# HGRN state in three groups, one query buffer, the gate row ahead of the norm's factor, and stores on SyncE in a two-layer backbone kernel

## The chip, the core and the metric

The kernel runs on one core of a Trainium2 chip. The core has TensorE (PE, matmuls into PSUM banks), VectorE (DVE), ScalarE (ACT), GpSimd (POOL) and SyncE (SP, which here issues DMAs), each with its own instruction stream; semaphores order them. The metric is the device time of one execution in microseconds (us); less is better. The profile is a recording of one such execution.

## The reference

The network has two layers on 512 latent tokens and 256 context tokens of width 1024, all float32. Layer 0 mixes tokens by bidirectional retention, layer 1 by HGRN2; each is followed by a ConvGLU channel mixer of hidden width 2816. Around every sub-layer stand two RMSNorms, and a shift, scale and gate from a condition vector (`mod`):

```python
u_l = rms_norm(h_l, norm_g[i, 0]) * (1.0 + sc1_l) + sh1_l
y_l = mixer(u_c, u_l, ...)
h_l = h_l + g1_l * rms_norm(y_l, norm_g[i, 1])
u_l = rms_norm(h_l, norm_g[i, 2]) * (1.0 + sc2_l) + sh2_l
h_l = h_l + g2_l * rms_norm(conv_ffn(u_l, ...), norm_g[i, 3])
```

HGRN2 has 8 heads of width 128. In each direction a state of 128x128 follows `S_t = diag(a_t) S_{t-1} + k_t v_t^T`, and the output is `o_t = S_t^T q_t`, context first, then latents from the context's last state; the outputs of both directions are summed. `q` is `silu` of a projection, `k` and `a` come from a sigmoid of another. Only the latents are returned, so layer 1 needs no context output.

## The kernel before

Matmuls are float32 in three passes: each operand is split into a high and a low part (`h..` by ScalarE's copy, `l..` by a subtraction on VectorE, line 94), and high x high, high x low and low x high are summed in PSUM. Weights come by DMA from SP into two raw buffers (`r..`), two high and two low ones. Activations `u` (`um`, `ue`) are kept transposed, features on the partitions. The stages are: retention with layer 0, its FFN, HGRN (about 1300 to 1740 us of the span), the second FFN (about 1800 to 2100), and an end.

PSUM has eight banks in two pools: six for projections and accumulation ("mm"), two for small products ("sc"). The order of PE's instructions is the program's order for the whole kernel. VectorE's and ScalarE's order is set by a scheduler when the kernel is built, except in the tails, below.

**HGRN.** `attend(h)` computes one head and yields weights; `weave` puts PE work of the next head's projections (for head 7: of `out1`, the output projection of heads 0 to 3) between its steps, a fixed number of columns (83000, for head 7 64000) by the weights, 37 in all. A head forms `A` (decay) and `K` for six blocks of 128 tokens, `Q` for both directions, the products of decays over 2, 4, ... 128 tokens (`T`, on GpSimd), and in seven levels `li` scales halves of `Q` and `K` by them (line 1209), copies them to `L` and multiplies them on PE (`hl`, line 1216) into the block-diagonal matrix `DG`. `hd` and line 1194 start `DG`. Then come the states: ten transposes of `K` (`ht`, copied to `KT` by ScalarE), ten products with `v` (`hc`, line 1240), each read by VectorE, which copies the first of a direction (`s`, line 1245) and chains the others (`S`, line 1248). They go in groups of 4, 1, 4, 1 through the two small banks. Last, `ho` sums over the four latent blocks the matrix part (line 1253) and both directions' state parts (1254, 1255), and `hn` starts the norm.

`Q` has two buffers, so the scheduler may begin the next head's `Q` (direction 0 on VectorE, line 1174; direction 1 on GpSimd, 1175) while this head's `ho` is not done. `k0`, the sum of both directions' `K`, is on GpSimd (1172).

**Tails.** Each stage ends in `tail`: the last output projection (`tl`), then `handover`, which per block of 128 tokens evacuates (line 421), squares and sums (424), forms the factor r (428 and a Newton step on VectorE), multiplies by r and the gate row `g` (448), adds to the residual `h` (451), forms the second norm's factor, scales (457, 459), transposes on PE in pairs of blocks (`tre`, `trm`, 473), modulates on ScalarE (482) and splits into u (489, 490). `tail` also holds the next stage's first projections (`ld`) in units of 24 matmuls. All steps are given to a `Plan` with an engine, a cost, dependencies and a rank; `Plan.run` simulates them on four engines with these costs and emits them in the order found, and for ScalarE and VectorE that order is kept. The last tail has no next stage: it works by halves of 512 columns (443, 445) and stores each half (446). `filler(n)` emits a part of the condition's modulation vectors, 16 matmuls `ada`, taken from a queue; the rest of the queue is done in the second FFN.

## Time and profile before

| | |
|---|---|
| median of 3 runs | 2158.03 us (2157.18 to 2159.58) |
| profiled execution | 2157.03 us, span 2155.3, granted clock 0.993 |
| busy: PE, DVE, ACT, POOL | 2096.5, 1340.6, 840.0, 304.5 us |
| PE busy in the span's 1300 to 1740 us (HGRN) | 418.99 of 440 us |
| PE busy in 1740 to 1800 us (HGRN's tail) | 53.63 of 60 us |
| PE busy in 1240 to 1300 us (first FFN's tail) | 60.00 of 60 us |

A row of the timeline has the start, the duration, the engine with the line, the operation, output and inputs, and the number of instructions that it stands for; brackets hold the idle time of the engine before it and what ended that. ACTq is ScalarE's queue of instructions that it issues but doesn't compute, DMAs among them. A row with x8 is eight instructions one after the other.

### The profile page before, as it was taken

The numbers are of one execution on the slowest core, as the hardware profiler recorded it, in microseconds if no ns is written. First come the engines' busy times: TensorE is split into PE (matmuls) and PEld (weight loads), VectorE is DVE, ScalarE is ACT, GpSimd is POOL, SyncE is SP. The second block draws the span as 40 slices with busy tenths as digits, with TensorE's granted clock in tenths as the row PEclk, the third lists the DMA queues.
The fourth block names the chain that finished last, engine by engine and source line by source line (L and its number), as shares of the span: only waits on it lengthen the run. The fifth ranks groups of instructions, "written<-read, shape, count | busy, mean of one in ns | idle before, by whom it ended". The sixth has DMA issues, their size and how long they took to land. (4 is left out here: it accounts for less than half of the span.)

```text
span 2155.3 us, 30784 instructions
## 1 busy us (share of the span) xinstructions
PE 2096.5 (97%) x12288; PEld 1767.7 (82%) x12288; DVE 1340.6 (62%) x2536; ACT 840.0 (39%) x1631; POOL 304.5 (14%) x383
## 2 busy tenths in 40 slices
PE   6999999999999999999999999999999889999997
PEld 5888888888888988888888889888888668888886
DVE  6866565663613777467676577777777765334545
ACT  5542342433523723322132166444443454333323
POOL 4622040310100000000000003333333310000000
PEclk9999999999999999999999999999999999999999
DMA  9122314234133223333333532212121253223232
GB/s 299 40 79 96 110 40 139 68 98 147 49 108 127 100 98 110 126 115 125 113 101 122 190 100 86 59 40 60 40 60 40 79 186 121 79 98 98 93 117 93
DMA packets 186608, 218.24 MB, mean 101 GB/s; under 512 B 6112, under 2 KB 157664, under 8 KB 185696
## 3 DMA queue, kind: packets, MB, share of 16 engines
q1 hardware_dynamic: 179280, 196.80, 27.9%
q0 software_dynamic: 2736, 13.11, 1.6%
q10 hardware_dynamic: 4448, 6.35, 0.9%
q8 instruction: 97, 1.59, 0.3%
q14 instruction: 47, 0.39, 0.1%
HBM read 200.90 MB, written 15.34 MB: 100 GB/s over the span
## 5 line engine op out<-in xcount | busy, mean ns | idle before, releaser
L121 PE MATMUL f<-um,hua 128*128 128x512 f32 (+1 forms) x960 | 258.2, 357 | 0.0
L121 PE MATMUL f<-um,huv 128*128 128x512 f32 (+1 forms) x960 | 255.9, 354 | 0.0
L264 DVE SCALAR_TENSOR_TENSOR rows<-rada,sc,rows 128x256 f32<-128x256 f32 x504 | 232.0, 485 | 5.4
L1059 PE MATMUL f<-hd,gt 128*128 128x512 f32 x720 | 228.3, 396 | 0.0
L121 PEld LDWEIGHTS f<-um,hua 128*128 128x128 f32 x960 | 169.7, 189 | 29.2 <-issue 3.8
L121 PE MATMUL hp<-ue,hhw 128*128 128x512 f32 (+1 forms) x672 | 192.1, 373 | 0.0
L121 PEld LDWEIGHTS f<-um,huv 128*128 128x128 f32 x960 | 170.1, 189 | 25.1
L121 PE MATMUL f<-um,lua 128*128 128x512 f32 (+1 forms) x480 | 170.2, 355 | 0.0
L121 PE MATMUL f<-um,luv 128*128 128x512 f32 (+1 forms) x480 | 169.9, 354 | 0.0
L1059 PEld LDWEIGHTS f<-hd,gt 128*128 128x128 f32 x720 | 135.1, 188 | 33.5 <-issue 0.8
L1059 PE MATMUL f<-ld,gt 128*128 128x512 f32 x360 | 142.3, 395 | 0.0
L121 PEld LDWEIGHTS hp<-ue,hhw 128*128 128x128 f32 x672 | 112.0, 190 | 17.8 <-issue 1.4
L817 PE MATMUL v<-hv,ua 128*128 128x512 f32 x384 | 120.6, 391 | 0.0
L121 PE MATMUL hp<-ue,lhw 128*128 128x512 f32 (+1 forms) x336 | 120.2, 358 | 0.0
L121 PEld LDWEIGHTS f<-um,lua 128*128 128x128 f32 x480 | 90.8, 189 | 13.0
L121 PEld LDWEIGHTS f<-um,luv 128*128 128x128 f32 x480 | 90.8, 189 | 12.6
L1031 DVE TENSOR_TENSOR c<-f,c 128x512 f32<-128x512 f32 (+1 forms) x60 | 36.1, 602 | 99.7 <-PE f L121 98.8
L985 PE MATMUL wo<-hwo,ogr 128*128 128x512 f32 x288 | 89.4, 391 | 0.0
L1018 ACT ACTIVATE c<-f,c_conv_b,c_conv_w 128x512 f32<-128x512 f32 (+1 forms) x60 | 42.1, 702 | 117.4 <-PE f L121 117.4
L817 PEld LDWEIGHTS v<-hv,ua 128*128 128x128 f32 x384 | 72.1, 188 | 15.3 <-issue 0.6
L93 ACT ACTIVATE hua<-rua 128x512 fp32r<-128x512 f32 x80 | 44.2, 621 | 102.2 <-DMA rua<-ffn_w_up 53.2
L451 POOL DMA_DIRECT2D h_dram<-hxe x6 | 3.2, 532 | 570.6 <-DVE yf L421 536.9
(503 smaller groups left out, 4820.7 us busy)
## 6 DMA issues: line engine op xcount, KB each, us to landing
rada<-ada_w SPq DMA_DIRECT2D x48, 1024.0 KB
rua<-ffn_w_up SPq DMA_DIRECT2D x20, 1024.0 KB
ruv<-ffn_w_up SPq DMA_DIRECT2D x20, 1024.0 KB
rd<-ffn_w_down SPq DMA_DIRECT2D x24, 768.0 KB
rhw<-hg_w_in SPq DMA_DIRECT2D x28, 512.0 KB
rv<-ret_w_in SPq DMA_DIRECT2D x8, 1024.0 KB
rg<-ret_w_in SPq DMA_DIRECT2D x8, 1024.0 KB
rqk<-ret_w_in SPq DMA_DIRECT2D x6, 1024.0 KB
```

The costliest lines, as they stand in the source:

```text
L93: self.nc.scalar.activation(hi, raw, AF.Copy)
L121: nc.tensor.matmul(o, a, b[:, s], start=(i == 0), stop=(i == n - 1))
L264: nc.vector.scalar_tensor_tensor(rows[:, v], raw[:, k], a, rows[:, v], ALU.mult, ALU.add)
L451: nc.vector.tensor_tensor(hb(b), hb(b), yb(b), ALU.add), nc.gpsimd.dma_start(hdst[ts], hb(b))))
L817: nc.tensor.matmul(ps, a, b, start=(c == 0 and k == 0 and z == 0), stop=(c == 1 and k == 3 and z == 2))
L985: nc.tensor.matmul(ps, l, r[:, k], start=(h == 0 and k == 0 and z == 0), stop=(h == 2 and k == 3 and z == 2))
L1018: nc.scalar.activation(c[:, s], ps, AF.Identity, bias=cb[:, i, mt : mt + 1], scale=w(1))
L1031: nc.vector.tensor_tensor(c[:, s], ps, c[:, s], ALU.mult)
L1059: nc.tensor.matmul(ps, l, r[:, k], start=(k1 + k == 0 and z == 0), stop=(k1 + k == nt - 1 and z == 2))
```

## The change

Six edits stand in the diff.

1. `handover`: two products of y with the gate row, 512 columns each, stand ahead of the factor r, and one operation `h = y*r + h` behind it, in place of `y*r*g` and an add. In the last tail this is by halves.
2. The last tail's stores are issued by SyncE.
3. In `attend` `Q` has one buffer, and one VectorE operation of 1024 columns forms both directions.
4. The states go in three groups: four of direction 0, four of direction 1, then the fifth of both. ScalarE copies them in three steps, the yields are 1, 1, 2, and `ho` takes the latent blocks in the order 1, 2, 3, 0 and direction 1 ahead of 0.
5. `out1` calls `filler` once, in its second half, and no longer twice. What it leaves comes in the second FFN's first unit.
6. The low parts of the last output weights (`lhwt`) are made by VectorE in place of GpSimd.

```diff
--- before.py
+++ after.py
@@ -436,19 +436,19 @@
                                                                             ALU.add))
             n = add("ACT", 0.28, [n], (-1,), lambda: start(r, ss[0][:, 2:3]))
             n = add("DVE", 0.55, [n], (-1,), lambda: self.newton(r[0], ss[0][:, 2:3]))
+            yg = [add("DVE", 0.69, [sq[c]], (pr, 1), lambda cs=half(c): nc.vector.tensor_tensor(
+                yb(b)[:, cs], yb(b)[:, cs], g[:, v, cs], ALU.mult)) for c in range(2)]
             if u is None:
                 for c in range(2):
                     cs = half(c)
-                    n = add("DVE", 1.35, [n], (pr, 2), lambda cs=cs: (
-                        nc.vector.scalar_tensor_tensor(yb(b)[:, cs], yb(b)[:, cs], r[0][:, 0:1], g[:, v, cs],
-                                                       ALU.mult, ALU.mult),
-                        nc.vector.tensor_tensor(hb(b)[:, cs], hb(b)[:, cs], yb(b)[:, cs], ALU.add),
-                        (nc.sync, nc.scalar)[c].dma_start(hdst[ts, cs], hb(b)[:, cs])))
+                    n = add("DVE", 0.75, [n, yg[c]], (pr, 2), lambda cs=cs: (
+                        nc.vector.scalar_tensor_tensor(hb(b)[:, cs], yb(b)[:, cs], r[0][:, 0:1], hb(b)[:, cs],
+                                                       ALU.mult, ALU.add),
+                        nc.sync.dma_start(hdst[ts, cs], hb(b)[:, cs])))
                 return None
-            n = add("DVE", 1.28, [n], (pr, 2), lambda: nc.vector.scalar_tensor_tensor(
-                yb(b), yb(b), r[0][:, 0:1], g[:, v], ALU.mult, ALU.mult))
-            n = add("DVE", 1.23, [n], (pr, 2), lambda: (
-                nc.vector.tensor_tensor(hb(b), hb(b), yb(b), ALU.add), nc.gpsimd.dma_start(hdst[ts], hb(b))))
+            n = add("DVE", 1.28, [n, *yg], (pr, 2), lambda: (
+                nc.vector.scalar_tensor_tensor(hb(b), yb(b), r[0][:, 0:1], hb(b), ALU.mult, ALU.add),
+                nc.gpsimd.dma_start(hdst[ts], hb(b))))
             n = add("ACT", 1.23, [n], (pr, 3), lambda: nc.scalar.activation(yb(b), hb(b), AF.Square,
                                                                            accum_out=ss[0][:, 3:4]))
             n = add("ACT", 0.28, [n], (-1,), lambda: start(q, ss[0][:, 3:4]))
@@ -1170,9 +1170,8 @@
             v = lambda n: vs[h - h % 2][1][n][:, (h % 2) * P : (h % 2) * P + P]
             k0 = tmp(f"k0{h}")
             nc.gpsimd.tensor_tensor(k0, K[:, 0, LAT], K[:, 1, LAT], ALU.add)
-            Q = tl([P, 2, TL], "Q", f"Q{h}", 2)
-            nc.vector.tensor_tensor(Q[:, 0], q, A[:, 0, LAT], ALU.mult)
-            nc.gpsimd.tensor_tensor(Q[:, 1], q, A[:, 1, LAT], ALU.mult)
+            Q = tl([P, 2, TL], "Q", f"Q{h}", 1)
+            nc.vector.tensor_tensor(Q, A[:, :, LAT], q.unsqueeze(1).broadcast_to([P, 2, TL]), ALU.mult)
             tots, cur = [A], A
             for li in range(7):
                 n = T >> (li + 1)
@@ -1224,35 +1223,34 @@
             order = ((4, 5, 0, 1, 2, 3), (5, 4, 3, 2, 1, 0))
             KT = tl([P, 2, 5, P], "KT", f"KT{h}", 1)
             S = tl([P, 2, 4, P], "S", f"S{h}", 1)
-            for d in range(2):
-                for j0, j1 in ((0, 4), (4, 5)):
-                    yield 1
-                    ps = self.sml(f"ht{h}{d}{j0}")
-                    for j in range(j0, j1):
-                        nc.tensor.transpose(ck(ps, j - j0), ck(K[:, d], order[d][j]), ident)
-                    nc.scalar.activation(KT[:, d, j0:j1], n4(ps)[:, : j1 - j0], AF.Copy)
-            for d in range(2):
-                st = tl([P, P], "s0", f"s0{h}{d}", 2)
-                for j0, j1 in ((0, 4), (4, 5)):
-                    yield 1
-                    ps = self.sml(f"hc{h}{d}{j0}")
-                    for j in range(j0, j1):
-                        nc.tensor.matmul(ck(ps, j - j0), KT[:, d, j], v(order[d][j]), start=True, stop=True)
-                    for j in range(j0, j1):
-                        c = ck(ps, j - j0)
-                        dst = st if j == 0 else S[:, d, j - 1]
-                        if j == 0:
-                            nc.vector.tensor_copy(dst, c)
-                        else:
-                            n = order[d][j]
-                            nc.vector.scalar_tensor_tensor(dst, st, tot[:, d, n : n + 1], c, ALU.mult, ALU.add)
-                        st = dst
+            trips = [[(d, j) for j in range(4)] for d in range(2)] + [[(0, 4), (1, 4)]]
+            for i, trip in enumerate(trips):
+                yield 1 + (i == 2)
+                ps = self.sml(f"ht{h}{i}")
+                for z, (d, j) in enumerate(trip):
+                    nc.tensor.transpose(ck(ps, z), ck(K[:, d], order[d][j]), ident)
+                nc.scalar.activation(KT[:, i, 0:4] if i < 2 else KT[:, :, 4], n4(ps)[:, : len(trip)], AF.Copy)
+            st = [tl([P, P], "s0", f"s0{h}{d}", 2) for d in range(2)]
+            for i, trip in enumerate(trips):
+                yield 1 + (i == 2)
+                ps = self.sml(f"hc{h}{i}")
+                for z, (d, j) in enumerate(trip):
+                    nc.tensor.matmul(ck(ps, z), KT[:, d, j], v(order[d][j]), start=True, stop=True)
+                for z, (d, j) in enumerate(trip):
+                    c = ck(ps, z)
+                    dst = st[d] if j == 0 else S[:, d, j - 1]
+                    if j == 0:
+                        nc.vector.tensor_copy(dst, c)
+                    else:
+                        n = order[d][j]
+                        nc.vector.scalar_tensor_tensor(dst, st[d], tot[:, d, n : n + 1], c, ALU.mult, ALU.add)
+                    st[d] = dst
             yield 1
             o = self.acc(f"ho{h}")
-            for n in range(4):
+            for n in (1, 2, 3, 0):
                 nc.tensor.matmul(ck(o, n), v(n), DG[:, n], start=True, stop=False)
-                nc.tensor.matmul(ck(o, n), S[:, 0, n], ck(Q[:, 0], n), start=False, stop=False)
-                nc.tensor.matmul(ck(o, n), S[:, 1, 3 - n], ck(Q[:, 1], n), start=False, stop=True)
+                nc.tensor.matmul(ck(o, n), S[:, 1, 3 - n], ck(Q[:, 1], n), start=False, stop=False)
+                nc.tensor.matmul(ck(o, n), S[:, 0, n], ck(Q[:, 0], n), start=False, stop=True)
             sq = tmp(f"hsq{h}")
             nc.scalar.activation(sq, o, AF.Square)
             yield 2
@@ -1278,7 +1276,7 @@
                     ms = slice(m * P, m * P + P)
                     yield from self.mm3g([(ps, ALL)], [(gh[0][:, k, ms], gh[2][:, k, ms], wh[:, k], wl[:, k]) for k in range(4)])
                     self.evac(y, m, c, ps, True)
-                    if m == 2:
+                    if c == 1 and m == 2:
                         self.filler(1)
                         yield 4096
             for h in range(4, 7):
@@ -1317,7 +1315,7 @@
             z = zn
         spl(7)
         ies.close()
-        w = [self.weights(wo[:, 4:8, c * 512 : c * 512 + 512], 4, 512, f"hwt{c}", nc.gpsimd) for c in range(2)]
+        w = [self.weights(wo[:, 4:8, c * 512 : c * 512 + 512], 4, 512, f"hwt{c}") for c in range(2)]
         pp = es.enter_context(tc.tile_pool(name="hpost", bufs=1))
         big = lambda s, dt, n: pp.tile(s, dt, tag="pb", name=n, bufs=2)
         outs = self.tail(w, lambda k: (gh[1][:, k], gh[3][:, k]), y, 4, lambda nb: mk(nb, y, big, tmp), nxt, 1)
```

The edits move instructions. The first place is VectorE in head 1 of HGRN, from the activation of the next head's query (`qg`) on; `s` and `S` are the states, `Q` the next head's query product, `T` the decay products, `lhw` low parts of the weights after next. Before:

```order
L1163 SCALAR_TENSOR_TENSOR qg_12227<-qg_12227,lb_oml,hp_12161 128x512
L1245 COPY s_12214<-hc_12218 128x128
L1174 TENSOR_TENSOR Q_12301<-qg_12227,AK_11790 128x512
L1248 SCALAR_TENSOR_TENSOR S_12177<-s_12214,T_1_11788,hc_12218 128x128
L1248 SCALAR_TENSOR_TENSOR S_12177<-S_12177,T_1_11788,hc_12218 128x128 x2
L1209 TENSOR_TENSOR Q_12301<-Q_12301,AK_11790 128x256
L1248 SCALAR_TENSOR_TENSOR S_12177<-S_12177,T_1_11788,hc_12237 128x128
L1209 TENSOR_TENSOR Q_12301<-Q_12301,AK_11790 128x256
L1209 TENSOR_TENSOR Q_12301<-Q_12301,T_2_12304 128x128x2
L1245 COPY s_12240<-hc_12244 128x128
L1209 TENSOR_TENSOR Q_12301<-Q_12301,T_2_12304 128x128x2
L1248 SCALAR_TENSOR_TENSOR S_12177<-s_12240,T_1_11788,hc_12244 128x128
```

With the change:

```order
L1163 SCALAR_TENSOR_TENSOR qg_12233<-qg_12233,lb_oml,hp_12168 128x512
L1243 COPY s_12219<-hc_12224 128x128
L1246 SCALAR_TENSOR_TENSOR S_12184<-s_12219,T_1_11795,hc_12224 128x128
L1246 SCALAR_TENSOR_TENSOR S_12184<-S_12184,T_1_11795,hc_12224 128x128 x2
L1243 COPY s_12220<-hc_12243 128x128
L1246 SCALAR_TENSOR_TENSOR S_12184<-s_12220,T_1_11795,hc_12243 128x128
L1246 SCALAR_TENSOR_TENSOR S_12184<-S_12184,T_1_11795,hc_12243 128x128 x2
L1246 SCALAR_TENSOR_TENSOR S_12184<-S_12184,T_1_11795,hc_12261 128x128 x2
L1174 TENSOR_TENSOR Q_12305<-AK_11797,qg_12233 128x1024
L94 TENSOR_TENSOR lhw_12326<-rhw_12322,hhw_12325 128x512
L1208 TENSOR_TENSOR Q_12305<-Q_12305,AK_11797 128x256 x2
L94 TENSOR_TENSOR lhw_12326<-rhw_12322,hhw_12325 128x512 x3
```

All operations on the states now stand together, and the query product with its level-0 trees stands behind them.

The second place is PE at the end of the first FFN, where the last pair of blocks is transposed (`tre`); `ld` are the first projections of HGRN, one PSUM bank or half bank a unit, `hv` the values' projection. Before:

```order
L121 MATMUL ld_10757<-ue_10437,lhl_10694 128x256
L473 MATMUL tre_10998<-c_ident,yf_7324 128x128 x4
L473 MATMUL tre_11003<-c_ident,yf_7324 128x128 x4
L121 MATMUL ld_10758<-ue_10436,hhl_10753 128x256
...
L121 MATMUL ld_10758<-ue_10437,lhl_10754 128x256
L473 MATMUL tre_11039<-c_ident,yf_7324 128x128 x4
L473 MATMUL tre_11045<-c_ident,yf_7324 128x128 x4
L121 MATMUL ld_10759<-ue_10436,hhl_10753 128x256
...
L121 MATMUL ld_10760<-ue_10436,hhl_10693 128x256
```

With the change:

```order
L121 MATMUL ld_10759<-ue_10443,lhl_10794 128x256
L473 MATMUL tre_11034<-c_ident,yf_7330 128x128 x4
L473 MATMUL tre_11039<-c_ident,yf_7330 128x128 x4
L121 MATMUL ld_10760<-ue_10442,hhl_10793 128x256
...
L121 MATMUL ld_10760<-ue_10443,lhl_10794 128x256
L473 MATMUL tre_11075<-c_ident,yf_7330 128x128 x4
L473 MATMUL tre_11081<-c_ident,yf_7330 128x128 x4
L121 MATMUL ld_10761<-ue_10442,hhl_10705 128x256
...
L121 MATMUL hv_11186<-hhv_11176,ue_10442 128x256
```

Before, one unit of 24 matmuls (`ld_10759`) stands between the last transposes and the context's two units (`ld_10760`), which read the last pair; with the change the context's units (`ld_10761`) follow at once.

The third place is ScalarE at the very end, from the first square of the last block on (`sqe` squares, `r2e` and `r3e` factors, `out` the result). Before:

```order
L424 ACTIVATE sqe_18106,ss3e_18101<-yf_16353 128x512
L424 ACTIVATE sqe_18122,ss2e_18076<-yf_16353 128x512
L428 ACTIVATE r2e_18125<-ss2e_18076,eps 128x1
L446 DMA out<-hxe_17964 128x512
L424 ACTIVATE sqe_18134,ss3e_18101<-yf_16353 128x512
L446 DMA out<-hxe_17964 128x512
L428 ACTIVATE r3e_18140<-ss3e_18101,eps 128x1
L446 DMA out<-hxe_17965 128x512 x2
```

With the change:

```order
L424 ACTIVATE sqe_18091,ss3e_18088<-yf_16337 128x512
L424 ACTIVATE sqe_18108,ss2e_18067<-yf_16337 128x512
L428 ACTIVATE r2e_18112<-ss2e_18067,eps 128x1
L424 ACTIVATE sqe_18120,ss3e_18088<-yf_16337 128x512
L428 ACTIVATE r3e_18126<-ss3e_18088,eps 128x1
```

The stores are gone from between the squares and the factor.

## The prediction

> **What bounds the kernel now.** I read the page first: its header and engine line.
>
> ```profile
> span 2155.3 us, 30784 instructions
> PE 2096.5 (97%) x12288; PEld 1767.7 (82%) x12288; DVE 1340.6 (62%) x2536; ACT 840.0 (39%) x1631; POOL 304.5 (14%) x383
> ```
>
> TensorE is busy 97% of the span. 58.8 us of the span are not matmul, and 12 of these lie behind the last matmul. The change takes no matmul away and adds none, so only PE's waits and that end can give anything. Next I read the waits of PE, summed by what ended them; columns are total us, number, longest.
>
> ```profile
> PE ho L1255 <- DVE S L1248: 8.4, 8, 2.4
> PE hc L1240 <- DVE S L1248: 8.3, 7, 1.2
> ...
> PE trm L473 <- DVE ss3m L435: 4.6, 1, 4.6
> ```
>
> Nearly everything that the change can touch is the state of the eight HGRN heads: PE waits 16.7 us in all on `S`, the running state that DVE makes out of the products in PSUM. Third is the timeline of head 1, whose rows show why DVE is late; brackets give idle time and what ended it.
>
> ```profile
> 1419.25 0.29 DVE L1245 COPY s<-hc 128x128 f32<-128x128 f32 x1
> 1419.41 1.28 POOL L1175 TENSOR_TENSOR Q<-qg,AK 128x512 f32<-128x512 f32 x1 [10.08 <-DVE qg L1163]
> 1419.45 1.79 DVE L1174 TENSOR_TENSOR Q<-qg,AK 128x512 f32<-128x512 f32 x1
> 1421.16 0.34 DVE L1248 SCALAR_TENSOR_TENSOR S<-s,T,hc 128x128 f32<-128x128 f32 x1
> 1421.54 0.73 DVE L1248 SCALAR_TENSOR_TENSOR S<-S,T,hc 128x128 f32<-128x128 f32 x2
> 1422.32 1.16 PE L1240 MATMUL hc<-hv,KT 128*128 128x128 f32 x8 [1.19 <-DVE S L1248]
> 1422.52 0.34 DVE L1248 SCALAR_TENSOR_TENSOR S<-S,T,hc 128x128 f32<-128x128 f32 x1
> 1423.82 1.45 POOL L1172 TENSOR_TENSOR k<-AK 128x512 f32<-128x512 f32 x1
> 1424.24 1.31 DVE L1209 TENSOR_TENSOR Q<-Q,T 128x256 f32<-128x256 f32 x1
> 1425.47 0.33 DVE L1248 SCALAR_TENSOR_TENSOR S<-s,T,hc 128x128 f32<-128x128 f32 x1
> 1425.85 1.18 DVE L1248 SCALAR_TENSOR_TENSOR S<-S,T,hc 128x128 f32<-128x128 f32 x3
> 1427.08 0.49 PE L1255 MATMUL ho<-Q,S 128*128 128x128 f32 x2 [0.85 <-DVE S L1248]
> ```
>
> Between the copy of the first chunk's state and the S operations DVE does the next head's query product. It runs 1.79 us because POOL's product of the other direction (1.28 us) runs beside it: DVE's starts 0.04 us behind POOL's and needs POOL's 1.28 and then some 0.5 of its own. PE's third group of hc needs the PSUM bank that the S operation of 1422.52 and those ahead of it still read; it waits 1.19 us. The same happens once more: k0's sum on POOL (1.45) stretches `Q<-Q,T` to 1.31, the last S start at 1425.85, and ho waits 0.85. That is 2.04 us a head.
>
> [...]
>
> **State and queries of heads 0 to 6.** With one query buffer the product of the next head cannot start before this head's ho has read the old one. So DVE's order puts all S operations together and the query behind them. The products go as 4, 4 and 2. I lay the S chain along PE's unchanged fill in head 1: first products end at 1418.7, second at 1421.0, third about 1423.1 (the two transposes' trips carry the same fill). A copy and three S operations take 0.29 + 0.34 + 0.73 = 1.4 us, so the first direction is through at 1420.65, the second at 1422.5, and the last two S at 1424.3. ho begins near 1424.2 and takes its d=1 states first; nothing waits. Gain: hc 8.3, and ho's 8.4 less the 0.97 of head 7 (row below), together 15.7 us. It could be less by some tenths a head if the last two S meet ho's second matmul: 13 to 15.7.
>
> What becomes late is the query chain. Rows of the same head, from ho's end to the first level product of the next head:
>
> ```profile
> 1429.19 0.39 PE L1255 MATMUL ho<-Q,S 128*128 128x128 f32 x2
> 1431.44 2.50 DVE L94 TENSOR_TENSOR lhw<-rhw,hhw 128x512 fp32r<-128x512 f32 x4 [4.41 <-ACT hhw L93]
> 1435.48 0.69 DVE L142 TENSOR_TENSOR whg<-rhg 128x512 f32<-128x512 f32 x1 [0.95 <-ACT rhg L137]
> 1436.82 1.02 DVE L1209 TENSOR_TENSOR AK<-AK 128x384 f32<-128x384 f32 x2
> 1438.35 0.85 DVE L1194 TENSOR_TENSOR DG<-hd,c_ident 64x256 f32<-64x256 f32 x2
> 1440.02 0.69 PE L1216 MATMUL hl<-L 128*64 128x64 f32 x16
> ```
>
> ho ends at T = 1429.6, and PE reaches hl0 at T+10.4. After the change DVE has behind T: the product of both directions, 1024 elements, which no row of this line shows; below is twice a 512 one (0.69 alone), above 1.4, I take 1.25. Then four weight splits (2.50), the four query trees of level 0 (1.6), qg and two whg operations (0.69 each), two AK (1.02), DG (0.85): together 9.3 us, and 0.85 for the meeting with k0 on POOL (the 1.31 row against 0.61 gives 0.7; 1.45 is its length). End T+10.1 to T+10.8. hl0 takes the bank that DG or the whg operation frees, so it waits 0 to 0.4 us, 0.9 where DVE stands for the whole of k0. Six heads: -1.2 us, from 0 to -5. Later levels have more fill ahead of them and catch up.
>
> **Head 7** has a different filler (the out projection of the first four heads), and one modulation step (16 ada matmuls) fewer.
>
> ```profile
> 1707.91 1.07 PE L216 MATMUL ada<-rada,sc 128*32 128x256 f32 x16 [1.50 <-issue]
> 1710.61 1.12 PE L1216 MATMUL hl<-L 128*64 128x64 f32 x16 [1.62 <-ACT rows L218]
> 1730.84 1.16 PE L1240 MATMUL hc<-hv,KT 128*128 128x128 f32 x8 [0.67 <-ACT KT L1233]
> 1737.03 0.49 PE L1255 MATMUL ho<-Q,S 128*128 128x128 f32 x2 [0.97 <-DVE S L1248]
> 1735.92 2.18 ACT L93 ACTIVATE hhwt<-rhwt 128x512 fp32r<-128x512 f32 x4
> L94 POOL TENSOR_TENSOR lhwt<-rhwt,hhwt x8: 1268/1280/1591, 1717.5 to 1740.3; 128x512 fp32r<-128x512 f32 x8
> ```
>
> The ada step's waits, 1.50 and 1.62, leave with it to the first unit of the second FFN, where weights come in time by about 1 to 2 us (nothing there, at worst -2). hl0 pays here as above, but two more splits stand in DVE's way: 2.5 us. The filler is 4096 columns shorter, so it runs out ahead of hc; there DVE's order weaves four splits `lhwt` of 0.69 between the S operations, which hang on ScalarE (2.18 for the four hhwt, which come behind its last evacuation). I get ho's end 3.9 us behind the last filler where now 0.67 + 0.97 are lost. So 1.50 + 1.62 + 0.67 + 0.97 = 4.8 go and 2.5 + 3.9 = 6.4 come: about -1.7, from -4 to +2. POOL's eight splits (1.28 each) cost nothing where they are now; DVE's cost what is counted here.
>
> **Gate row ahead of the factor.** A block had a scalar-tensor-tensor of 1024 and an add of 1024 behind r (the planner's 1.28 + 1.23). Now two products of 512 stand ahead of r and one operation of 1024 behind it: DVE does the same 2.5 us and the path behind r is 1.2 us shorter. That makes pairs ready sooner, and the planner, which sets ACT, DVE and PE by its own prices, puts the parts in another order. HGRN's end (the 4.60 us on ss3m) should gain 4 us on its first pair. But the second pair's transposes now stand one unit of 24 matmuls later, and the next unit needs them; laying the rows by hand I get 1800.5 for an end that is 1800.4 now: 0, from -2 to +3.
>
> The two other tails lose nothing now. At the FFN's end the order of PE is: transposes of the last pair, one unit that doesn't need them, the context unit that does. After the change that unit stands ahead of the transposes.
>
> ```profile
> 1308.69 1.03 PE L473 MATMUL tre<-c_ident,yf 128*128 128x128 f32 x8
> 1309.33 1.93 ACT L482 ACTIVATE hxe<-tre,mod,mv1A 128x256 f32<-128x256 f32 x4 [0.78 <-PE tre L473]
> 1311.14 1.16 ACT L489 ACTIVATE ue<-hxe 128x512 fp32r<-128x512 f32 x2
> 1312.51 1.15 ACT L93 ACTIVATE hhv<-rhv 128x512 fp32r<-128x512 f32 x2 [0.21 <-PE ld L121]
> ```
>
> From the start of the transposes to the first half of u it takes 1311.14 + 0.58 - 1308.69 = 3.0 us, as ACT makes all four modulations first; interleaved it is near 2.1. PE has 1.03 of transposes to do in it and then stands: 1.1 to 2.0 us. At HGRN's start the four hhv copies (2.2 us) go ahead of the last modulations in ACT's order: 2.9 in place of 1.1. With small ones of 0.3 to 0.6 at the first pairs: -5 us for both tails, from -1 (the parts come together better than by hand) to -8.
>
> **Stores on SyncE.** The code names two queues in turn, but the name is looked up when the step is emitted, after the loop; in the timeline all eight output stores stand in ScalarE's queue.
>
> ```profile
> 2143.33 0.69 DVE L421 TENSOR_TENSOR yf<-tl,yf 128x512 f32<-128x512 f32 x1 [0.18 <-PE tl L526]
> 2145.43 0.34 ACTq L446 DMA_DIRECT2D out<-hxe  x1
> 2145.82 0.63 ACT L424 ACTIVATE sqe<-yf 128x512 f32<-128x512 f32 x1 [3.25 <-DVE hxe L445]
> 2148.16 0.34 ACTq L446 DMA_DIRECT2D out<-hxe  x1
> 2148.54 0.29 ACT L428 ACTIVATE r3e<-ss3e,eps 128x1 f32<-128x1 f32 x1 [2.00 <-DVE hxe L445]
> 2151.62 0.69 DVE L445 TENSOR_TENSOR hxe<-hxe,yf 128x512 f32<-128x512 f32 x1
> ```
>
> The store of 2145.43 waits for DVE and holds the square of 2145.82 back, that of 2148.16 holds r3e. Without them: evacuation to 2144.0, two operations of block 2 to 2145.45 (0.74 each), the square beside them, ss3e, r3 0.3 by 2145.95, one gate product that is left to 2146.25, Newton 0.6, two final operations of 0.75: 2148.35, where now the last ends at 2151.62 + 0.69 = 2152.31. 4.0 us, between 3.5 and 4.5; the tail from store to span end stays as it is.
>
> **Sum**, against the profiled execution's 2157.03: -15.7 + 1.2 + 1.7 + 0 + 5 - 4.0 = -11.8, that is 2145.2. The median of the runs is 1.0 above that execution, so 2146.
>
> **The rivals.**
>
> *The tails hold.* The planner prices a waiting unit too, and PE has not waited in the first two tails under its old order. If they cost 1 and HGRN's gains 2: 2146 - 6 = 2140. For it: prices (0.95 a pair of modulations, 0.62 a copy) are near the rows. Against: no unit stands between the transposes and their reader any more.
>
> *The single query buffer takes the state's gain back in part.* If lhv's splits, which wait for a DMA and for ScalarE, stand ahead of the level-0 trees and each head's hl0 waits 1.5 in place of 0.2, heads 1 to 6 give 8 us back: 2154. For it: hl0 has no reserve now. Against: its ho ends 2 us sooner, and the fill ahead of hl0 is what it was. [...]
>
> *Slower: DVE's chain becomes the bound of a head.* Place: from ho's end to hl1, where Q, four trees, four splits and the norm all stand on one engine behind T. Price: the sum above if each Q operation met a POOL copy of L or k0, 0.5 each for six, 3 us a head more, for six heads 18: 2164. It decides from 2.0 us a head (12 us over six). Against it: DVE is busy 62% of the span, POOL loses its 1.28 product and its splits, and such meetings are in the present rows already.
>
> *It does not do what it says.* The S chain could still wait, since DVE's order is fixed before the run: if ho waits 0.85 a head as now, 2152. The order shows nothing between the S operations, so I give it little.
>
> **How the numbers follow.** Forecast 2146 (own range 2142 to 2151): 0.48. Tails hold, 2140: 0.20. Query chain, 2154, with the ho variant: 0.23. Slower: 0.09, of which half reaches beyond 2162. What a measurement of this kernel can tell from no change is 0.2%, 4.3 us: below 2153.7 is faster, above 2162.3 slower. Faster: 0.48 + 0.20 + 0.15 of the third = 0.83; same 0.12; slower 0.05. The range takes the low end of the second case and the high end of the third: all good ends together would be 2134, all bad ones 2163, neither likely; 2136 to 2156.
>
> **What would show it.** Right: no PE wait on S in heads 0 to 6 (16.7 us now, at most 4 after, all in head 7); PE's waits in the first two tails, on the modulated input, of 2 us each where there are none; the last matmul to the span's end 8 us, not 12; DVE's query product of 1.25 us right behind ho. hl0 waits would name DG or whg. Wrong: if S waits stay, or hl0 waits pass 1 us a head, the step on heads is wrong; if PE's tails show no wait, the planner's order was right and my layout by hand too pessimistic; if POOL's k0 runs beside the trees and each takes over 1 us, the third case has it.

## The result and the profile after

The changed kernel takes 2144.73 us (median; 2144.12 to 2146.05), the kernel before 2158.44 (2157.18 to 2159.58) beside it: ratio 0.9931, 95% interval 0.992 to 0.9943. The profiled span went from 2155.3 to 2142.4 us. The forecast was 2146, own range 2142 to 2151.

PE's waits after the change, columns as before (us in all, times, longest):

```profile
PE hc L1238 <- DVE S L1246: 3.3, 1, 3.3
PE hl L1215 <- DVE DG L1193: 2.5, 1, 2.5
...
PE ld L121 <- ACT ue L489: 2.2, 1, 2.2
PE trm L473 <- ACT hxm L482: 2.0, 2, 1.7
PE ld L121 <- ACT um L489: 1.5, 3, 0.7
...
PE hn L131 <- ACT hsq L1255: 0.7, 1, 0.7
PE trm L473 <- DVE yh L457: 0.6, 1, 0.6
...
PE hd L1188 <- POOL k L1172: 0.6, 1, 0.6
PE ht L1231 <- DVE DG L1219: 0.5, 1, 0.5
```

The two rows on S in heads 0 to 6 are gone: hc's 8.3 us and ho's. What stands there now is new, or was smaller: 3.3 and 2.5 us in head 7, 0.7 us on `um` at the end of the first tail (the other 0.8 of its row are in HGRN's tail) and 2.2 us on `ue` at the end of the second. The 4.6 us on ss3m became 2.0 us on the modulation and 0.6 on `yh`.

To see where the time went, the starts of the same PE instructions are compared in the two timelines.

| from, to | before | after | difference |
|---|---|---|---|
| span's start to the first `trm` (retention's end) | 702.0 | 702.9 | +0.9 |
| first `trm` to first `hv` (the first two tails, first FFN) | 616.2 | 620.6 | +4.4 |
| first `hv` to hn of head 0 | 60.2 | 57.6 | -2.6 |
| hn of head 0 to hn of head 6 | 316.5 | 301.1 | -15.4 |
| hn of head 6 to hn of head 7 | 45.3 | 47.8 | +2.5 |
| hn of head 7 to the start of the last matmul | 402.7 | 404.4 | +1.7 |
| last matmul to span's end | 12.4 | 8.0 | -4.4 |
| sum | 2155.3 | 2142.4 | -12.9 |

The same place of VectorE in the head whose ho ends at 1379.9 (head 0), after:

```profile
1374.71 0.73 DVE L1246 SCALAR_TENSOR_TENSOR S<-S,T,hc 128x128 f32<-128x128 f32 x2
1376.54 0.61 DVE L1246 SCALAR_TENSOR_TENSOR S<-S,T,hc 128x128 f32<-128x128 f32 x2 [1.09 <-PE hc L1238]
1379.98 1.23 DVE L1174 TENSOR_TENSOR Q<-AK,qg 128x1024 f32<-128x1024 f32 x1 [2.84 <-PE ho L1253]
1383.24 3.42 DVE L94 TENSOR_TENSOR lhv<-rhv,hhv 128x512 fp32r<-128x512 f32 x3
1389.39 0.85 DVE L1193 TENSOR_TENSOR DG<-hd,c_ident 64x256 f32<-64x256 f32 x2
```

The last S operations wait for PE's products and not the other way round. The query product stands right behind ho. GpSimd beside it:

```profile
1383.14 1.28 POOL L1202 TENSOR_SCALAR L<-Q 128x256 f32<-128x256 f32 x2 [1.03 <-DVE Q L1208]
1384.39 1.73 POOL L1172 TENSOR_TENSOR k<-AK 128x512 f32<-128x512 f32 x1
```

Three splits take 3.42 us, while two copies to L (1.28 us) and k0 (1.73 us) run on GpSimd at the same time; a split with no GpSimd instruction beside it takes 0.69 us in this execution. DG ends at 1390.24, 10.4 us behind ho's end, and PE's hl0 starts at 1390.39. It waited 0.15 us for DG, which is too short for the list of waits; the hl0 behind ho of heads 2 and 4 does the same.

VectorE in head 7, from the first state's copy on:

```profile
1720.32 0.29 DVE L1243 COPY s<-hc 128x128 f32<-128x128 f32 x1 [4.70 <-PE hc L1238]
1720.65 0.69 DVE L94 TENSOR_TENSOR lhwt<-rhwt,hhwt 128x512 fp32r<-128x512 f32 x1
1721.26 0.34 DVE L1246 SCALAR_TENSOR_TENSOR S<-s,T,hc 128x128 f32<-128x128 f32 x1
1721.51 0.68 DVE L94 TENSOR_TENSOR lhwt<-rhwt,hhwt 128x512 fp32r<-128x512 f32 x1
1722.57 1.29 DVE L94 TENSOR_TENSOR lhwt<-rhwt,hhwt 128x512 fp32r<-128x512 f32 x2
1723.78 0.34 DVE L1246 SCALAR_TENSOR_TENSOR S<-s,T,hc 128x128 f32<-128x128 f32 x1
```

Four splits of the last output weights stand between the state operations, and hc, which needs the bank, waits 3.25 us.

At the start of HGRN, two rows of PE, then three of ScalarE:

```profile
1313.84 1.03 PE L473 MATMUL tre<-c_ident,yf 128*128 128x128 f32 x8
1318.50 0.38 PE L121 MATMUL ld<-ue,hhl 128*128 128x256 f32 x1 [2.20 <-ACT ue L489]
1313.92 2.20 ACT L93 ACTIVATE hhv<-rhv 128x512 fp32r<-128x512 f32 x4 [0.21 <-PE ld L121]
1316.02 1.91 ACT L482 ACTIVATE hxe<-tre,mod,mv1A 128x256 f32<-128x256 f32 x4
1317.82 1.15 ACT L489 ACTIVATE ue<-hxe 128x512 fp32r<-128x512 f32 x2
```

The last transposes run at 1313.84, but their modulations start at 1316.02, behind the four hhv copies; the context's unit waits 2.20 us for what they make.

The end, on VectorE:

```profile
2134.87 0.69 DVE L421 TENSOR_TENSOR yf<-tl,yf 128x512 f32<-128x512 f32 x1
2135.48 1.40 DVE L445 SCALAR_TENSOR_TENSOR hxe<-yf,r2e,hxe 128x512 f32<-128x512 f32 x2
2136.80 0.15 DVE L435 TENSOR_TENSOR ss3e<-ss3e 128x1 f32<-128x1 f32 x1
2136.87 0.68 DVE L439 TENSOR_TENSOR yf<-yf,hxe 128x512 f32<-128x512 f32 x1
2138.04 1.41 DVE L445 SCALAR_TENSOR_TENSOR hxe<-yf,r3e,hxe 128x512 f32<-128x512 f32 x2
```

Block 2's operations follow the evacuation at once, one gate product is left for the time of the factor, and the last operation ends at 2139.45, 4.6 us behind the last matmul, where it was 9.0.

### The profile page after: what moved, and what is told of

The parts are those of the page before. It is cut to its first block, busy times and chain, and to the rows that moved or that the text cites. A ratio compares the mean times of both kernels' runs of the same rounds, so it can differ in the third digit from the quotient of the medians.

```text
span 2142.4 us, 30771 instructions
## 1 busy us (share of the span) xinstructions
PE 2098.6 (98%) x12288; PEld 1770.1 (83%) x12288; DVE 1344.5 (63%) x2560; ACT 839.4 (39%) x1623; POOL 287.8 (13%) x367
## 3 DMA queue, kind: packets, MB, share of 16 engines
q8 instruction: 97, 1.59, 0.3%
## 4 chain that ended last, share of the span: by engine, by line
PE 92%; DVE 4%; ACT 2%; DMA 1%; issue 0%; POOL 0%; SPq 0%; DVEq 0%
PE f L121 26%; PE f L1059 12%; PE hp L121 8%; PE v L817 6%; PE tl L526 5%; PE wo L985 5%; PE ld L121 4%; PE g_l L121 4%; PE av L868 3%; PE hv L121 3%; PE qk_l L121 3%; PE g_c L121 2%; PE s L121 2%; PE hl L1215 2%; PE qk_c L121 2%; PE hwo L121 1%
## 5 line engine op out<-in xcount | busy, mean ns | idle before, releaser
L1202 POOL TENSOR_SCALAR L<-Q 128x256 f32<-128x256 f32 x112 | 59.6, 545 | 221.3 <-DVE Q L1174 125.2
L817 PEld LDWEIGHTS v<-hv,ua 128*128 128x128 f32 x384 | 72.1, 188 | 15.4 <-issue 0.6
```

Source lines behind the costliest of these rows:

```text
L817: nc.tensor.matmul(ps, a, b, start=(c == 0 and k == 0 and z == 0), stop=(c == 1 and k == 3 and z == 2))
L1202: nc.gpsimd.tensor_scalar(vw(L[:, 1])[:, :, hf[1 - d]], vw(Q[:, d])[:, :, hf[1 - d]], 1.0, 0.0, ALU.mult, ALU.add)
```

## The experiments

The main theory after the comparison: the place of the query work in VectorE's order makes the S waits, and the query edit alone takes them away. The gate row's edit costs the first two tails as much as the whole end gains. The rivals: the three groups do it; the tails lose time for another reason. Since single executions also differ ahead of the changed code (the first `trm` starts anywhere from 701.9 to 706.1 us in these runs), parts are read by the steps of the table. "Mean step" is the mean of the five steps from hn to hn between heads 0 and 5; a time marked "one" is of a single execution. The runs were made in groups, and the kernel before took 2158.44 us beside the changed one, 2158.00 beside the next four of the table, 2160.55 beside the four after those and 2160.96 beside the last three. Times of different groups are therefore comparable to about 3 us only.

| kernel | us | mean step | head 6 to 7 | hn 7 to last matmul | last matmul to end |
|---|---|---|---|---|---|
| before | 2158.44 | 52.49 | 45.31 | 402.7 | 12.4 |
| changed | 2144.73 | 50.15 | 47.79 | 404.4 | 8.0 |
| q1_only | 2144.49 (one) | 50.19 | 46.29 | 404.6 | 12.4 |
| groups_only | 2151.33 (one) | 51.40 | 44.26 | 403.8 | 12.4 |
| stores_only | 2160.22 (one) | 52.49 | 46.89 | 404.2 | 10.2 |
| gate_last | 2140.34 (one) | 50.15 | 47.93 | 405.3 | 7.9 |
| pool_splits | 2145.81 (one) | 50.16 | 45.49 | 403.7 | 8.0 |
| filler_twice | 2138.77 (one) | 50.16 | 44.04 | 402.3 | 8.0 |
| gate_last_pool | 2138.81 | 50.15 | 45.50 | 406.2 | 8.0 |
| query_end_only | 2138.66 | 50.19 | 46.17 | 404.0 | 8.0 |
| gate_last_filler | 2135.75 | 50.17 | 44.06 | 404.6 | 8.0 |
| gate_4blocks | 2134.31 | 50.18 | 43.81 | 400.6 | 8.0 |
| early_k0 | 2128.95 | 50.00 | 40.41 | 400.6 | 7.9 |

**The query edit alone.**

```diff
-            Q = tl([P, 2, TL], "Q", f"Q{h}", 2)
-            nc.vector.tensor_tensor(Q[:, 0], q, A[:, 0, LAT], ALU.mult)
-            nc.gpsimd.tensor_tensor(Q[:, 1], q, A[:, 1, LAT], ALU.mult)
+            Q = tl([P, 2, TL], "Q", f"Q{h}", 1)
+            nc.vector.tensor_tensor(Q, A[:, :, LAT], q.unsqueeze(1).broadcast_to([P, 2, TL]), ALU.mult)
```

> The kernel before with only the query edit: one query buffer and one VectorE product of 1024 columns; state groups stay 4, 1, 4, 1. Theory (place of the query work): with one buffer VectorE's order has all S operations together, so PE's waits on S in heads 0 to 6 (15.7 us before) fall under 2 us in all, and the step from one head's hn to the next falls from 52.5 us to about 50.3; time near 2143 to 2146, because tails and end stay as before but no tail loses. Rival (the three groups do it): the fifth product of a direction still holds a bank alone, hc keeps about 1 us of wait a head, and the step stays above 51.3 us; time 2150 or more.

PE's waits of this kernel on DG and on S:

```profile
PE hl L1215 <- DVE DG L1193: 2.9, 4, 2.4
...
PE ho L1254 <- DVE S L1247: 0.9, 2, 0.6
```

The step is 50.19 us, the changed kernel's 50.15, with groups of 4, 1, 4, 1. ho waits 0.9 us in two heads; of hl's 2.9 us 2.4 are head 7's, and three heads wait 0.16. The theory holds: the query edit alone takes the S waits away. It holds two things, the single buffer and the product of both directions on VectorE, and no run takes them apart. By the code it is the single buffer that keeps the product behind ho, but that is argued and not shown. That q1_only's time equals the changed kernel's is chance in its parts: its first two tails lose nothing and its end gains nothing.

**The state edit alone.** The trips, the order of ho and the yields of the change in the kernel before, with two query buffers.

> The kernel before with only the state edit: three groups and the new order of ho; two query buffers, one product on GpSimd. Theory: VectorE's order still puts the query product and its level-0 trees among the S operations, so PE waits on S stay, 1.5 to 3 us a head, and the time is 2155 to 2165. Rival: the three groups free the banks sooner and the waits go whatever VectorE does beside; step from hn to hn near 50.3 us, time 2143 to 2146.

```profile
PE ho L1253 <- DVE S L1247: 9.6, 7, 2.1
```

Neither expectation held. hc no longer waits; ho waits 1.25 us in each of six heads and 2.1 in head 6, where I expected 1.5 to 3 a head. The step falls by 1.09 of 2.34 us. So the groups take away the bank's wait whatever VectorE does, and the query edit takes away both. With the query edit the groups add nothing in the mean step; they add 0.6 us in the step from head 5 to head 6 (50.9 us in q1_only, 50.3 in the changed kernel), where q1_only's ho still waits 0.28.

**The stores alone.**

```diff
-                        (nc.sync, nc.scalar)[c].dma_start(hdst[ts, cs], hb(b)[:, cs])))
+                        nc.sync.dma_start(hdst[ts, cs], hb(b)[:, cs])))
```

> The kernel before with only the last tail's stores on SyncE. Theory: the squares and r3e no longer stand behind stores that wait for VectorE; by the rows the last VectorE operation moves from 9.0 us behind the last matmul's end to about 7.0, a gain of 2.0 us, and the other 2.4 us of the 4.4 that the changed kernel gained at the end belong to the gate row. Rival: ScalarE's stores were no hold, or SyncE's land later: under 0.5 us.

The end is 2.2 us shorter, as expected (2.0), so the other 2.2 of the change's 4.4 are the gate row's. But this execution is the slower one, and its code is the same up to the end. Part of that is visible: the same wait of 2.35 us in head 6 is followed by halved clock here and not in the kernel before. The rows below cut both executions along the grid of 3.41 us on which their clock changed (the last section describes it). Columns are length, PE busy, granted clock, DMA share, GB/s. This kernel, where the wait lies in one stretch:

```profile
1688.54:1691.95 3.41, 1.05 (x8) 1.00 0.00 0
1691.95:1695.36 3.41, 3.41 (x16) 0.50 0.00 0
```

The kernel before, where the same wait is shared by two:

```profile
1686.28:1689.69 3.41, 2.55 (x15) 1.00 0.02 5
1689.69:1693.10 3.41, 1.92 (x17) 1.00 0.00 0
1693.10:1696.52 3.42, 3.42 (x18) 1.00 0.00 0
```

hn of head 5 to hn of head 6 is 55.7 us against 54.1; head 7 and its tail each lost another 1.5 us that the edit cannot touch, and each has 3.4 us more of halved clock than in the kernel before.

**The gate row in the last tail only.** The two products and the single operation behind the factor stay in the branch `u is None`; the three other handovers have the two operations of before.

> The changed kernel, with the gate row's edit only in the last tail; the three other handovers are as before. Theory: the planner's order of the first two tails lost 4.4 us and the third about 0.5 (PE events of the two traces); these come back, the waits on um and ue at the ends of the first two tails (1.0 and 2.5 us) are gone, time 2139 to 2141. Rival: the lost time in the tails has another cause (arrival of weights, the clock): the waits stay, time 2144 to 2146.

As expected: no wait on `um` or `ue` is left in the first two tails, and from the first `trm` to the first `hv` it is 617.0 us, close to the 616.2 of before. The single time of 2140.34 is 4.4 us below the changed kernel's; 3.6 of them are this step.

**Head 7: who splits the last weights, and how often the modulation step is called.**

```diff
-        w = [self.weights(wo[:, 4:8, c * 512 : c * 512 + 512], 4, 512, f"hwt{c}") for c in range(2)]
+        w = [self.weights(wo[:, 4:8, c * 512 : c * 512 + 512], 4, 512, f"hwt{c}", nc.gpsimd) for c in range(2)]
```

> The changed kernel, with the low parts of the last output weights back on GpSimd. Theory: head 7's wait of hc on S (3.25 us, and some 2 us of halved clock behind it) is made by the four lhwt splits that VectorE's order weaves into the S operations; without them it is under 0.7 us, and the step from head 6's hn to head 7's hn falls from 47.8 us to 43 to 45. Rival: GpSimd's splits hold VectorE (its operations ran 1.3 us for 0.4 beside them in the kernel before), so the levels of head 7 come late and hl waits take it back: step 46.5 us or more.

```profile
1719.94 0.78 PE L1215 MATMUL hl<-L 128*64 128x64 f32 x16 [1.32 <-DVE DG L1219]
1727.92 0.71 PE L1238 MATMUL hc<-hv,KT 128*128 128x128 f32 x4 [0.71 <-DVE S L1246]
```

hc's wait falls from 3.25 to 0.71, the step from 47.79 to 45.49; hl now waits 1.32 on DG late in the head. Both effects are there, and the first is larger; the step is just above the range of the theory. Up to 1.7 of its 2.3 us, an estimate from half of a stretch of 3.41 us, are the halved clock behind hc's wait, which is gone with it: the first pairs of ho matmuls behind the wait take 0.39 us here and 0.63 in the changed kernel. The single time of 2145.81 shows nothing of it, since this execution reached the first `trm` 3.2 us later than the changed kernel's and lost 1.5 us more by the first `hv`, where its clock was halved.

```diff
-                    if c == 1 and m == 2:
+                    if m == 2:
```

> The changed kernel, with the modulation step called in both halves of out1 as before. Theory: 16 ada matmuls (1.07 us) come back into head 7 and go from the second FFN, which cancels; VectorE's order now has the last four lhwt splits behind the S operations, so hc's wait of 3.25 us falls below 1 us, but the ada step's own waits (1.50 and 1.62 us before) return in part: head 7's step 45 to 48 us, last matmul within 1.5 us of the changed kernel's. Rival: the edit itself is what removed 3.1 us of waits, so putting it back costs 3 us: step 50 us or more.

Two waits in head 7 of this kernel:

```profile
1693.26 0.69 PE L1215 MATMUL hl<-L 128*64 128x64 f32 x16 [2.44 <-DVE DG L1193]
1700.07 0.69 PE L1215 MATMUL hl<-L 128*64 128x64 f32 x16 [1.53 <-ACT rows L218]
```

The step is 44.04, below the range, though it holds 1.07 us more matmuls: hc's wait is gone, since the last four splits stand behind the S operations, and the ada step's own waits came back with 1.53 of 3.1 us. The clock stayed whole in this head, where the changed kernel's was halved for 6.8 us, so a part of the 3.75 us is that. The last matmul starts 5.3 us ahead of the changed kernel's, where 1.5 either way was expected.

**Sums of parts.** gate_last with the splits on GpSimd:

> The changed kernel, with the gate row's edit in the last tail alone and the splits on GpSimd. Theory, both parts added: 4.4 us from the tails and 3 us from head 7, 2137 to 2139 us. Rival (the parts were measured with the clock's luck in them): 2140 to 2143.

2138.81 (2136.67 to 2139.31), ratio to before 0.9899 (0.9884 to 0.9913): the theory holds. The kernel before with only the query edit and the last tail's two edits:

> The kernel before with only the query edit and, in the last tail, the gate row and SyncE stores; state groups 4, 1, 4, 1, splits on GpSimd, modulation step in both halves. Theory: all of the gain is in these two, since the single query buffer alone gave steps of 50.2 us: 13.5 from the query edit and 4.4 at the end, 2140 to 2141 us. Rival: the three groups are needed with them for the hl0 waits of 0.16 us and head 6: 2142 or more.

2138.66, ratio 0.9902 (0.9885 to 0.9918), better than either expectation. These two edits give more than the whole change: the rest of it costs about 6 us in the tails and head 7.

**The gate row where four blocks are handed over, and there alone.** filler_twice with the edit in HGRN's tail and the last one (`nb == 4`), and, beside it, in the last one alone:

> The changed kernel with the modulation step in both halves of out1 and the gate row's edit only in the two tails of four blocks (HGRN's and the last); the first two tails as before. Theory, parts added: filler_twice had 2138.8 with tails that lose 4.4 us, so 2133.5 to 2135.5. Rival: the start of the program and the halved clock differ from run to run by 2 to 4 us, and part of filler_twice's gain was that: 2136 to 2139.

> The same, with the gate row's edit in the last tail alone, so that the two differ in HGRN's tail only. Theory: from head 7's hn to the second FFN's first matmul the gate row's order is worth 1 us (it loses 4.1 us in waits where the old loses 6.1, but the last projections wait more), so this kernel is 0.5 to 1.5 us slower than gate_4blocks. Rival (my sum by hand): 0, within 0.4 us.

2134.31 (ratio 0.9879, 0.9864 to 0.9893) and 2135.75 (0.9887, 0.987 to 0.9903). The first is as expected. The two differ by 1.4 us in their medians, in the expected direction, but the intervals overlap and the timed runs alone don't settle it. In the profiled executions HGRN's tail differs by 4.0 us (400.6 against 404.6), of which some 1.6 are matmul waits and the rest goes with the clock: over the 60 us from hn 7 on the granted clock is 0.97 with the gate row ahead and 0.89 without. The other runs point the same way. From hn of head 7 to the second FFN's first matmul the eight profiled executions with the old order of this tail take 60.3 to 62.6 us, 61.7 in the mean, and the five with the new one 58.2 to 60.8, 59.4 in the mean.

**k0 earlier.** gate_4blocks, with k0's sum emitted in the projection right behind K:

```diff
+                        if m == 1:
+                            z["k0"] = tmp(f"k0{h}")
+                            nc.gpsimd.tensor_tensor(z["k0"], K[:, 0, LAT], K[:, 1, LAT], ALU.add)
...
-            k0 = tmp(f"k0{h}")
-            nc.gpsimd.tensor_tensor(k0, K[:, 0, LAT], K[:, 1, LAT], ALU.add)
+            k0 = z["k0"]
```

> gate_4blocks with k0, the sum of both directions of K on GpSimd, emitted in the projection right after K, so that it no longer runs beside VectorE's splits behind ho. Theory: k0 (1.72 us there) holds VectorE's splits and makes hd wait 0.59 us; without it the splits take about 1 us less, hl0's wait in head 7 falls from 2.44 us to 0.8 to 1.6, and the halved clock behind it may go with it: 1 to 3 us faster than gate_4blocks. Rival: the copies to L hold the splits as much as k0 does: hl0's wait stays above 2 us, no gain.

Two VectorE rows behind head 0's ho, and PE's hl0 in head 7:

```profile
1377.48 0.82 DVE L94 TENSOR_TENSOR lhv<-rhv,hhv 128x512 fp32r<-128x512 f32 x1 [0.64 <-ACT hhv L93]
1378.89 2.32 DVE L94 TENSOR_TENSOR lhv<-rhv,hhv 128x512 fp32r<-128x512 f32 x3
1685.82 0.69 PE L1224 MATMUL hl<-L 128*64 128x64 f32 x16 [1.41 <-DVE DG L1202]
```

The three splits take 2.32 us in place of 3.42, hl0 waits 1.41 in place of 2.44, hd no longer waits, and behind this wait the clock stays whole:

```profile
1685.80:1687.80 2.00, 1.98 (x22) 1.00 0.05 16
1687.80:1689.80 2.00, 2.00 (x22) 1.00 0.00 0
```

2128.95 us (2127.77 to 2130.03), ratio to before 0.9855 (0.984 to 0.9869): 5.4 us below gate_4blocks, more than the 1 to 3 expected. In the profiled executions head 7's step is 3.4 us shorter, with 3.4 us less of halved clock in it, and the five steps 0.9. Something I hadn't counted helps: K's level-0 trees scale K in place, so they had to wait until k0 had read K; in this kernel's timeline they no longer stand behind ho. This is the fastest kernel of the study, 32.0 us below the kernel before that ran beside it (2160.96).

## Why the prediction was right, step by step

- **States and queries, heads 0 to 6** (forecast 15.7 us less, 1.2 back for hl0; measured 18.0 less). The mechanism was right: all S waits went. One row was misread: the third hc of head 1 starts at 1422.32, so what held its bank was the pair of S operations from 1421.54 to 1422.27, and not the one of 1422.52, which starts later. VectorE's chain behind ho was forecast to end at T+10.1 to 10.8 and ended at T+10.4 in heads 0, 2 and 4 and at T+11.0 in 1, 3 and 5. hl0 came at T+10.5 and T+10.8 and waited 0.15 us for DG behind the first three and not behind the others. early_k0, where it does not wait, is 0.8 us shorter from the first `hv` to hn of head 6, so about that much was paid where 1.2 was forecast. The states alone then gave some 18.8 us, 3.1 more than the sum had. The rows show one way in which the term was too small: a wait cost more than its row's idle time. In head 1 before, the matmul ahead of the third hc starts at 1420.74 and the next of its kind follows 0.23 us behind in the unbroken stream, so hc was due at 1420.97 and came at 1422.32: 1.35 us for a row that says 1.19. Fourteen waits at 0.16 us each would make 2.2 of the 3.1 us; this is an estimate from one of them, and the rest isn't explained.
- **Head 7** (forecast 1.7 us lost; measured 2.5 on top of 1.07 us of matmuls that left it, 3.6 in all). hl0's 2.5 us was forecast and measured 2.46; for ho I had 3.9, and hc waits 3.25 at its place. The waits of the step come to 6.8 us against 4.8 before. What the sum did not have is the clock: behind each of these two waits it was granted by half for 3.4 us, where the kernel before has one such stretch (behind the 1.50 and the 1.62), and one stretch more is up to 1.7 us, an estimate from half of its 3.41 us.

```profile
1692.70:1694.70 2.00, 2.00 (x20) 0.68 0.00 0
1694.70:1696.70 2.00, 2.00 (x6) 0.50 0.00 0
1696.70:1698.70 2.00, 2.00 (x22) 0.96 0.00 0
1724.40:1726.40 2.00, 1.97 (x9) 0.50 0.67 203
1726.40:1728.40 2.00, 2.00 (x15) 0.71 0.93 321
1728.40:1730.40 2.00, 1.31 (x10) 1.00 0.00 0
```

- **HGRN's tail** (forecast 0; measured +0.5 from hn of head 7 to the second FFN's first matmul, 60.3 to 60.8). PE's waits there fell from 6.1 to 4.1 us, but the clock stayed at half from 1758 to 1768, 10.2 us, where it was 6.8 us before. My sum by hand was right by luck and for the wrong reason: it had later transposes in place of the clock, and in the mean of the 13 profiled executions the new order is 2.3 us faster here (59.4 against 61.7).
- **The first two tails** (forecast 5 us lost, from 1 to 8; measured 4.4). Both mechanisms are in the rows: the context's unit straight behind the transposes, and the four hhv copies (2.20 us) ahead of the last modulations. The waits are 0.7 + 0.3 and 2.2 + 0.3, where about 2 us each was expected; the small ones that I added at the first pairs did not come.
- **The end** (forecast 4.0, from 3.5 to 4.5; measured 4.4). Half is the stores', half the gate row's, which the forecast did not separate.
- **The second FFN** (forecast 0): its weights came in time; it took over the 16 matmuls and is 1.3 us longer for it.
- **The sum** of 11.8 us against 12.9 in the profiled spans and 13.7 in the medians. Two errors offset each other: 3.5 us too little from the heads, 2 us too little lost in head 7. A third part, 0.9 us ahead of the first tail, lies in code that the change doesn't touch. That the total came this close is therefore in part luck.
- **The rivals.** That the tails hold fell: they lost 4.4 us. That the single buffer gives the gain back fell for heads 1 to 6 (hl0 waits 0.15 us in three of them and not 1.5), and is right in head 7. The slower case fell: it needed 2.0 us a head, and early_k0 puts it at some 0.2. Its mechanism, GpSimd beside VectorE behind ho, is real: the last of the three splits takes 1.78 us beside k0 and 0.68 without it, 1.1 us where 0.85 was charged. That the S operations still wait fell, since no such wait is left in heads 0 to 6.

## What to carry to other kernels

Where two engines hand a chain back and forth, a second buffer for the next round's work can hurt: a scheduler that may start that work early puts it into the chain. Give it one buffer, or emit it behind the chain, and look then at what the late start collides with: here k0 on GpSimd, whose move gave another 5.4 us in the medians. A planner's order that is made with costs near the measured ones still loses where a unit that needs a result is placed straight behind the work that makes it; one that gains at a tail with four blocks can lose at one with six, so such an edit is tried at each place alone. Read a single execution by its steps between the same instructions, since its total also holds a start and a clock that the edit doesn't touch.

## What the hardware showed that I had not expected

The granted clock of PE was halved behind waits of little more than 2 us (2.08 us in groups_only, 2.46 in the changed kernel), but not behind every wait of that length (2.44 in filler_twice). In the clock records of these 13 executions the clock is 1.00 or 0.50 and nothing between. The halved stretches ahead of the last matmul last 3.41 us or two, three or four times that, and within one execution they all lie on one grid of 3.41 us. The grid is not at the same place in every execution: a halved stretch begins at 1710.17 us in the kernel before and at 1693.44 in the changed one, 4.9 lengths of the grid apart. With the grid laid over each execution, from 60 us ahead of head 7's hn to 75 us behind it, all 29 stretches of whole clock in which PE was idle for 1.79 us or more were followed by a halved one, and none in which it was idle for less than 1.47 us. Between these values three were and nine were not. No run here tries gap lengths one by one, so the bound between 1.47 and 1.79 us is left open.

So the same wait can do both. hl0's wait of 2.44 to 2.46 us in head 7 was followed by half clock in seven of nine executions; in filler_twice and gate_last_filler a line of the grid cuts it, and no stretch there holds more than 1.59 us of idle time. Behind the 2.2 us at HGRN's start the clock stayed whole in the changed kernel (1.67 us in one stretch) and was halved in pool_splits (2.30) and filler_twice (1.65). The shortest single wait with half clock behind it is one of 2.08 us in groups_only's head 6; behind 1.41, and behind the 1.19 and 0.85 of each head before, it never halved. Matmuls of 128x512 start 0.43 us apart in the halved stretch of the changed kernel's head 7 and 0.23 us apart behind it, so the price of such a stretch is by estimate up to half its length, 1.7 us. A later wait can hide it: head 7's step is 43.81 us in gate_4blocks with one and 44.04 in filler_twice without, as the next wait fell from 1.53 to 0.59 us.

Some of VectorE's operations took longer while GpSimd's ran beside them. Three splits took 3.42 us beside 3.0 us of GpSimd work and 2.32 with the 1.73 us of k0 taken away; no run shows what decides which operations this holds for. The split beside k0 ended 0.55 us behind k0's end, as the query product of the kernel before ended 0.55 us behind GpSimd's.
